# The mixer of an encoder layer: squares summed through transposes, values scaled behind theirs, a new order of work

## The chip, the cores and the metric

The kernel runs on one core of one Trainium2 chip. The core has five engines that work side by side, each through its own queue of instructions in program order: TensorE (matmuls and transposes, written to PSUM), VectorE, ScalarE, GpSimd, and SyncE, which here only issues DMAs. They wait for one another through semaphores. PSUM has eight banks of 128 partitions by 512 float32 numbers. The metric is the time of one execution in microseconds (us), the median of several runs; lower is better.

## What is computed

One layer of an encoder, for 512 positions of 1024 channels in float32: a half-step gated feed-forward network, a mixer, another feed-forward network, a last norm. Only the mixer is touched. It reads, cut to what matters:

```python
def rms_norm(x, g):
    return x * rsqrt(mean(x * x, axis=-1) + EPS) * g

h = rms_norm(x, mix_norm)
u = h @ w_in                  # fourier group (512) | q (8 x 64) | k (2 x 64) | v (2 x 64)
f_out = fourier_mixer(u[..., :512])
q = rms_norm(q.reshape(b, s, 8, 64), q_norm)     # each head by itself
k = rms_norm(k.reshape(b, s, 2, 64), k_norm)
q, k = apply_axial_rope(q), apply_axial_rope(k)
p = softmax(q @ k.T / 8)      # four query heads share one key and value head
a_out = p @ v
x = x + concat([f_out, a_out]) @ w_out
```

There are two norms in a row for q and k: that of x over 1024 channels (its factor, one number a position, is called 1/rms below, `n1.r` in the kernel) and that of each head over its 64 channels.

## The kernel before

Activations lie transposed: channels on the partitions, the 512 positions along a row. Every matmul operand is split into a high and a low part, and a product is three matmuls (high with high, high with low, low with high). The feed-forward networks run before and after the mixer, with TensorE at work without a break.

The mixer is written as some 630 small named operations, and a string `ORDER` (line 47) names them in the order in which they are issued; each engine's queue is this order cut to its own operations, on all five engines. Names that matter below:

- `wk.r`, `wk.h`, `wk.l` (and `wq0` to `wq3`, `wv`, `f0` to `f3`, `fw`, `o0` to `o7`): a weight's load by SyncE into one of three raw buffers, its high part (a cast, mostly on ScalarE) and its low part (a subtraction on VectorE). High and low go into one of three pairs of ring slots, which come free when TensorE is done with the weight that was there.
- `k.0` to `k.7`, `q0.0` to `q3.7`, `v.0` to `v.7`: the eight steps of a projection, three matmuls each.
- `k.sq`, `q0.sq` ...: ScalarE squares the projected bank. `pq`: the squares summed over each head's 64 channels. `s0`, `s1`, `s2`: the sum made into a factor (`s1` is a power of -1/2 on GpSimd).
- `sw`, `sd`, `rc`, `rs`: the rotary step. `ah`, `al`, `bh`, `bl`: the queries' high and low parts. `kw`, `kp`, `km`: the key's factor spread over its channels, transposed, multiplied in. `k0.0` to `k1.3`: the key's parts.
- `vt`, `vp`: the values scaled, transposed to positions on the partitions; `v0.h`, `v0.l`, `v1.h`, `v1.l`: their parts.
- `n1.c`, `n1.m`, `n1.p`: the squares of x summed over the channels, made a mean, and a power -1/2 on GpSimd. `n1.t`, `n1.b`: 1/rms transposed to a row that lies on all partitions, copied to SBUF.
- `s`, `m`, `e`, `t`, `h`, `l`, `v` with three digits (queries, head, block): scores, their maximum (VectorE), exponential (ScalarE), four transposes, the high and low part, product with the values. `o`, `z`, `r`: the attended values gathered, the softmax sums (their reciprocal `z0.r`, spread by GpSimd in `z0.w`, transposed in `z0.p`), the result.
- `f00.0` ... , `map`, `d`, `c`: the Fourier branch; `y0.0` to `y7.7`: the output projection, with the start of the next norm.

Before, the projected q, k and v are not yet multiplied by 1/rms. A head's factor is worked out from the summed squares: times 1/rms twice, divided by 64, EPS added, power -1/2, times 1/rms and (for q) 1/8. So `s0` and `s2` need `n1.p`, and `vt` needs the row of `n1.b`. The sums of squares are matmuls with two columns: the squares are the weights, `halves` (ones in one half of the partitions, zeros in the other) or `ones` the moving operand.

Banks are handed out in the order of the string (`bank_for` takes the first spare one, `read` gives it back), so the order also decides which operation waits for whose bank. Temporary tiles rotate in the same way.

Of the kernel before, what the change touches and what calls it, by code (L numbers as in the profile page):

```python
# [6 lines left out]
F32 = mybir.dt.float32  # L7
# [14 lines left out]
HD = 64  # L22
EPS = 1e-6
# [27 lines left out]
wq3.h q0.bl pos vt wq3.l k1.2 q0.pq q1.1 q1.2 q0.s0 k1.0 k1.1 k1.3 vp q1.3 q1.4 q1.5 q1.6 q1.7 k0.0 k0.2 v0.h  # L51
k0.1 f1.r k0.3 s001 s000 q0.s1 q1.sw q0.s2 v0.l f0.h q1.sd s002 s010 m001 q1.sq q1.pq s003 q2.0 q2.1 q2.2 q2.3
m002 m010 q1.s0 e010 q2.4 q2.5 e001 q2.6 f0.l v1.h q2.7 m003 m000 e002 e003 s011 e000 t000 t001 h001 q1.rc
q1.rs v1.l q3.0 q2.sw f1.h f1.l m011 l001 h000 l000 q2.sd q2.sq t002 s012 m012 h002 fw.r l002 q1.ah q1.al
q2.rc q3.1 q3.2 q3.3 q3.4 q3.5 q3.6 q3.7 q1.bh q1.bl e012 s100 e011 s102 q2.rs q3.sw q3.rc s013 m013 t003 f2.h
q2.bh q1.s1 q1.s2 v000 v001 f00.0 f2.l v002 q3.sq m100 q2.pq e013 q3.sd m102 h003 l003 t010 q2.ah q2.al e100
t013 e102 s101 m101 e101 f00.1 q2.bl f00.u t011 h011 v003 q2.s0 s103 t012 q3.rs q3.bh l011 f02.0 m103 s110
q3.pq h010 l010 v010 v011 o00.c o00.a s201 h012 l012 s111 e103 q3.s0 t100 q3.bl h013 l013 q3.ah t102 h100 m110
v012 v013 o01.c f3.r f02.1 h102 l100 s112 q3.s1 m111 e111 o01.a t101 s113 z0.r z0.w l102 f01.0 h101 e110 m112
z0.p l101 q2.s1 v100 e112 v101 m113 e113 s203 s200 t103 r0.m r0.h f02.e h103 f02.h z1.r q3.s2 q2.s2 m200 z1.w  # L60
e200 l103 r0.l t110 h110 t112 q3.al f01.1 v102 m203 v103 o10.c m201 f01.u l110 o0.r s202 m202 h112 f03.0 o10.a
f03.1 f3.h v110 f03.e t113 e201 t111 f03.h s210 f3.l f03.l f10.0 f10.1 o1.r l112 s211 h111 l111 v111 h113 v112
e203 f10.u l113 s212 m210 m211 e202 t200 m212 t202 s300 f02.l e210 t201 h202 l202 e211 v113 m300 h200 f12.0
h201 l200 l201 f12.1 fw.h fw.l s213 m213 e212 s301 t203 o11.c z1.p v200 v201 v202 o11.a r1.m f12.e e213 t210
s303 h203 l203 e300 t211 h210 f11.0 h211 r1.h m301 l210 l211 s302 f12.h t212 v203 e301 m303 o20.c f13.0 m302
r1.l e302 f12.l s311 f11.1 h212 o20.a m311 z2.r t213 v210 f13.1 l212 s310 o0.h o0.l o3.r map0 o2.r h213 f11.u
l213 e303 t300 t302 f13.e o1.h m310 o1.l v211 v212 v213 t301 f13.h e310 f13.l d00 o21.c o21.a d10 map1 h302
z2.w l302 z2.p map0.h map0.l t303 h300 e311 s312 map1.h l300 v300 r2.m d20 h303 o2.h m312 d01 map1.l s313 d11
h301 l303 l301 v301 m313 d0.h d0.l v302 v303 c0.s e312 e313 t312 t311 o2.l d1.h d1.l o30.c c0.q c0.c d21 h312
# [16 lines left out]
def encoder(ctx, tc, A, out):  # L86
# [660 lines left out]
    with tc.tile_pool(name="mix", bufs=1) as mp, tc.tile_pool(name="mixt", bufs=1) as mt:  # L747
# [132 lines left out]
        def heads_ops(name, t, factor):  # L880

            v = sc[:, :, 2 * t : 2 * t + 2]
            rx = n1.r.unsqueeze(2).to_broadcast([P, 4, 2])

            @op(f"{name}.pq")
            def _():
                banks[f"pq{name}"] = pq = bank_for(f"pq{name}")
                for c in range(4):
                    nc.tensor.matmul(
                        pq[:, 2 * c : 2 * c + 2], sqs[name][:, c * P : (c + 1) * P], halves, start=True, stop=True  # L890
                    )

            @op(f"{name}.s0")
            def _():
                pq = banks[f"pq{name}"][:, 0:8].rearrange("p (c t) -> p c t", t=2)
                nc.vector.tensor_tensor(out=v, in0=pq, in1=rx, op=ALU.mult)
                read(f"pq{name}")
                nc.vector.tensor_tensor(out=v, in0=v, in1=rx, op=ALU.mult)
                nc.vector.tensor_scalar(out=v, in0=v, scalar1=1.0 / HD, scalar2=EPS, op0=ALU.mult, op1=ALU.add)

            @op(f"{name}.s1")
            def _():
                nc.gpsimd.tensor_tensor(out=v, in0=v, in1=mhalf.rearrange("p (c t) -> p c t", t=2), op=ALU.pow)

            @op(f"{name}.s2")
            def _():
                nc.vector.scalar_tensor_tensor(out=v, in0=v, scalar=factor, in1=rx, op0=ALU.mult, op1=ALU.mult)

        qa, qb = {}, {}

# [52 lines left out]
        @op("vt")  # L963
        def _():
            rots["v"] = tp.tile([P, S], F32, tag="g", name="vt")
            nc.vector.tensor_tensor(out=rots["v"], in0=banks["v"], in1=n1.rb, op=ALU.mult)
            read("v")

        @op("vp")
        def _():  # L970
            banks["vp"] = vp = bank_for("vp", 2)
# [3 lines left out]
        def value_ops(v):  # L975


            def own():
                return banks["vp"].rearrange("p (c v e) -> p c v e", c=4, v=2)[:, :, v, :]

            op(f"v{v}.h")(lambda: nc.scalar.copy(vst[:, v, :, 0, :], own()))

            @op(f"v{v}.l")
            def _():
                lows(vst[:, v, :, 1, :], own(), vst[:, v, :, 0, :])
                read("vp")

        for v in range(2):
            value_ops(v)

        for i in range(4):
# [279 lines left out]
        scale = HD**-0.5  # L1275
# [3 lines left out]
        heads_ops("k", 0, 1.0)  # L1279
        key_ops()  # L1280
        for t in range(4):
            query_ops(t)
            heads_ops(f"q{t}", t + 1, scale)
# [18 lines left out]

        @op("n1.c")
        def _():
            banks["ss"] = bank_for("ss")
# [17 lines left out]
        def _():  # L1323
            nc.scalar.copy(n1.rb, banks["rp"])
            read("rp")


        @op("pos")
        def _():
# [237 lines left out]
```

## Time and profile before

| | |
|---|---|
| median of 3 runs | 826.89 us (826.85 to 827.06) |
| the profiled execution | 827.06 us |
| its span in the profile | 824.8 us |
| granted TensorE clock, mean | 0.999 |
| TensorE busy | 816.9 us |
| VectorE busy | 639.2 us |
| ScalarE busy | 464.6 us |
| GpSimd busy | 30.7 us |

The span is the time from the first to the last instruction; the execution has 2.3 us around it. Engines are named PE (TensorE's matmuls), PEld (its weight loads, which overlap them), DVE (VectorE), ACT (ScalarE), POOL (GpSimd) and SP (SyncE) in the profile, and L889 is line 889 of the kernel. A row of a group reads: line, engine, operation, output<-inputs, shapes, xcount | busy time in all, mean ns of one | idle time of the engine before them, and who ended it. A row of the timeline reads: start, duration, engine, line, operation. A row of waits reads: who <- waited for whom: time in all, times, longest. Consecutive operations of an engine overlap in part, so what one costs in a full queue is the distance from its start to the next start.

### The profile page before, as it was taken

To read this page: it belongs to the slowest core of one execution; us is meant where nothing else is said; L and a number is where in the kernel's file an instruction comes from. 1 tells how busy PE (TensorE), PEld (TensorE's weight loads), DVE (VectorE), ACT (ScalarE), POOL (GpSimd) and SP (SyncE) were. 2 spreads that over 40 slices of the span, in tenths; PEclk is the share of its full clock that TensorE was granted. 3 is DMA by queue.
4 is the path that set the end of the run, shared out by engine and by line. 5 is a ranking of instruction groups with operands and counts; after the bars stand their busy time and mean duration, and the time that the engine had idled before them with its cause. 6 is when DMAs were issued, how large, how long until landed. Compare 5 with 4: busy or idle time off the path is not lost.

```text
span 824.8 us, 13679 instructions
## 1 busy us (share of the span) xinstructions
PE 816.9 (99%) x5406; PEld 750.4 (91%) x5406; DVE 639.2 (78%) x1005; ACT 464.6 (56%) x778; POOL 30.7 (4%) x34
## 2 busy tenths in 40 slices
PE   9999999999999999999999999999999999999997
PEld 7889999899989998888999888899988999899986
DVE  7998896489756947699998488998955896479574
ACT  7764664167524645677786357556632674256462
POOL 0110000000000000221100000100000000000001
PEclk9999999999999999999999999999999999999999
DMA  7664322323242213522020224453232332422222
GB/s 256 180 145 173 122 91 77 122 103 141 78 140 102 64 55 115 184 93 77 26 77 27 82 97 116 119 163 123 90 122 94 128 116 63 138 103 97 69 77 103
DMA packets 31168, 89.58 MB, mean 109 GB/s; under 512 B 3712, under 2 KB 8832, under 8 KB 31104
## 3 DMA queue, kind: packets, MB, share of 16 engines
q1 hardware_dynamic: 27776, 82.61, 29.2%
q0 software_dynamic: 2608, 5.12, 3.4%
q8 instruction: 42, 0.69, 0.3%
q10 hardware_dynamic: 720, 0.98, 0.3%
q14 instruction: 22, 0.18, 0.1%
HBM read 84.24 MB, written 2.10 MB: 105 GB/s over the span
## 4 chain that ended last, share of the span: by engine, by line
PE 92%; DVE 5%; issue 1%; ACT 0%; DMA 0%; POOLq 0%; POOL 0%; DVEq 0%; ACTq 0%
PE dn L183 25%; PE r L419 23%; PE q L419 12%; PE gu L183 8%; PE mix L183 7%; PE p L419 6%; PE gu L708 3%; PE mix L1219 1%; PE mix L1176 1%; DVE mx L1156 1%; PE mix L1073 1%; DVE pl L127 1%; PE mix L1015 1%; PE mix L1016 1%; PE mix L1014 1%
## 5 line engine op out<-in xcount | busy, mean ns | idle before, releaser
L419 PE MATMUL r<-rt,ring 128*128 128x256 f32 x1686 | 209.2, 276 | 0.0
L183 PE MATMUL dn<-at,ring 128*128 128x512 f32 x900 | 203.3, 381 | 0.5 <-DVE ring L127 0.4
L419 PEld LDWEIGHTS r<-rt,ring 128*128 128x128 f32 x1686 | 200.3, 188 | 0.8
L183 PEld LDWEIGHTS dn<-at,ring 128*128 128x128 f32 x900 | 168.0, 188 | 29.8 <-DVE ring L127 1.6
L419 PE MATMUL q<-rt,ring 128*128 128x256 f32 x840 | 106.6, 276 | 0.0
L127 DVE TENSOR_TENSOR ring<-s,ring 128x1024 fp32r<-128x1024 f32 x70 | 85.4, 1220 | 24.1 <-ACT ring L378 20.8
L419 PEld LDWEIGHTS q<-rt,ring 128*128 128x128 f32 x840 | 100.4, 188 | 0.0
L543 DVE SCALAR_TENSOR_TENSOR gx<-dn,gx 128x512 f32<-128x512 f32 x61 | 41.9, 688 | 67.6 <-PE dn L183 67.6
L378 ACT CAST ring<-s 128x1024 fp32r<-128x1024 f32 x70 | 73.5, 1050 | 28.0 <-PE p L419 13.7
L169 ACT CAST ring<-raw_dn 128x768 fp32r<-128x768 f32 (+3 forms) x58 | 45.2, 783 | 71.3 <-PE dn L183 62.1
L127 DVE TENSOR_TENSOR ring<-raw_dn,ring 128x768 fp32r<-128x768 f32 (+3 forms) x58 | 51.5, 891 | 5.6 <-PE r L419 4.4
L419 PE MATMUL p<-rt,ring 128*128 128x256 f32 x420 | 53.3, 276 | 0.0
L127 DVE TENSOR_TENSOR ring<-raw_g,ring 128x1024 fp32r<-128x1024 f32 x35 | 42.7, 1219 | 11.1 <-PE p L419 10.2
L419 PEld LDWEIGHTS p<-rt,ring 128*128 128x128 f32 x420 | 50.2, 188 | 0.0
L183 PE MATMUL gu<-ring 128*128 128x512 f32 x216 | 48.9, 381 | 0.0
L183 PEld LDWEIGHTS gu<-ring 128*128 128x128 f32 x216 | 40.4, 188 | 6.9
L378 ACT CAST ring<-raw_g 128x1024 fp32r<-128x1024 f32 x35 | 36.8, 1051 | 16.0 <-DMA raw_g<-in_wgu 8.8
L427 ACT COPY p<-r 128x256 f32<-128x256 f32 x35 | 12.9, 370 | 46.7 <-PE r L419 46.3
L451 ACT ACTIVATE g<-g 128x512 f32<-128x512 f32 x35 | 22.2, 633 | 23.4 <-DVE g L450 23.1
L387 ACT CAST ring<-raw_u 128x512 fp32r<-128x512 f32 x35 | 21.8, 624 | 16.6 <-PE q L419 16.0
L255 POOL TENSOR_TENSOR r<-ms,mhalf 128x4 f32<-128x4 f32 (+1 forms) x4 | 4.3, 1072 | 659.5 <-DVE ms L248 659.5
L464 DVE TENSOR_TENSOR u<-g,u 128x512 f32<-128x512 f32 x35 | 24.0, 685 | 6.1 <-ACT u L463 6.0
(271 smaller groups left out, 1323.1 us busy)
## 6 DMA issues: line engine op xcount, KB each, us to landing
raw_g<-in_wgu SPq DMA_DIRECT2D x35, 512.0 KB, 3.6
raw_u<-in_wgu SPq DMA_DIRECT2D x35, 512.0 KB, 4.3
raw_dn<-in_wd SPq DMA_DIRECT2D x40, 384.0 KB, 3.1
raw_gu<-in_wgu SPq DMA_DIRECT2D x12, 512.0 KB, 3.5
raw_o<-in_wo SPq DMA_DIRECT2D x8, 512.0 KB, 3.5
raw_dn<-in_wd SPq DMA_DIRECT2D x8, 448.0 KB, 3.4
raw_wq<-in_wins SPq DMA_DIRECT2D x4, 512.0 KB, 5.1
raw_f<-in_winf SPq DMA_DIRECT2D x4, 512.0 KB, 4.1
```

Source lines behind the costliest of these rows:

```text
L127: nc.vector.tensor_tensor(out=lo, in0=src, in1=asf(hi), op=ALU.subtract)
L169: nc.scalar.copy(hi[:, :n, :], raw[:, :n, :])
L183: nc.tensor.matmul(ps, a, b, start=first and b is mhi and a is whi, stop=last and a is wlo)
L378: nc.scalar.copy(hi, src)
L387: nc.scalar.copy(hi, src)
L419: nc.tensor.matmul(ps[:, t], a[:, ks], b[:, i, t], start=first and i == 0 and o == 0, stop=i == KH - 1 and o == 2, skip_group_check=not first,
L427: nc.scalar.copy(t, ps)
L451: nc.scalar.activation(b["g"], b["g"], AF.Silu)
L464: nc.vector.tensor_tensor(out=u, in0=b["g"], in1=u, op=ALU.mult)
L543: nc.vector.scalar_tensor_tensor(out=x[d][:, t], in0=ps[:, t], scalar=0.5, in1=x[d][:, t], op0=ALU.mult, op1=ALU.add)
L708: nc.tensor.matmul(turned(pss[c]), w[:, k % 2, c], turned(m[k]), start=k == 0 and m is hh and w is hi, stop=k == KD - 1 and w is lo,)
L1014: nc.tensor.matmul(ps, hh[k][:, cs], whi[:, a, :], start=k == 0, stop=False)
```

## The change

The sums of squares no longer go through two-column products. TensorE transposes the squares, four blocks of 128 x 128 into one bank, and VectorE sums along the row: in `pq` and `s0` for each head's 64 channels, in `n1.c` and `n1.m` for the norm of x (that is, 128 of the partial sums, over which the eight blocks of channels have been added up before).

The head's factor is worked out without 1/rms: sum of squares + 64 EPS (mean of x squared + EPS), power -1/2. This is the whole factor of q; for k a factor of 8 is applied in `kw`. So the steps `s2` go, and `s0` needs only `n1.m` (which also writes the new tile `eps_ms`), not `n1.p`.

The values are copied by ScalarE (`vt`), transposed, and then multiplied by 1/rms (`vs`, VectorE), which is now a number of each partition; `v.h` and `v.l` split both heads at once, from SBUF instead of from PSUM. The row of 1/rms (`n1.t`, `n1.b`) goes.

The string `ORDER` is replaced by another; it has 625 names for 633. Its first part, where it differs most in kind:

```diff
-wk.r wq0.r wv.r wk.h wk.l wq0.h k.0 cos k.1 wv.h wq1.r wq0.l k.2 k.3 wv.l wq2.r k.4 k.5 k.6 k.7 k.sw k.rc k.rs
-q0.0 f0.r q0.1 q0.2 q0.3 k.sq n1.c n1.m wq1.h n1.p wq1.l q0.4 q0.5 q0.6 q0.7 wq2.h q0.rc v.0 wq3.r q0.sw wq2.l
-q1.0 k.pq k.s0 f2.r q0.rs q0.ah v.1 v.2 v.3 q0.sq q0.bh k.s1 k.s2 kw q0.al v.4 v.5 v.6 kp km n1.t n1.b v.7
...
+wq0.r wk.r wv.r wk.h pos wq0.h wk.l k.0 k.1 k.2 k.3 wq1.r k.4 wq1.h k.5 k.6 k.7 wv.h n1.c k.sq wq0.l q0.0
+q0.1 q0.2 cos k.pq wq1.l n1.m q0.3 q0.4 k.sw f3.r q0.5 wv.l wq2.r k.s0 q0.6 k.s1 k.rc q0.7 q1.0 wq2.h k.rs
+q1.1 q1.2 q1.3 q0.rc q0.sq kw f1.r wq2.l kp v.0 q0.sw km k0.2 q0.pq k0.0 k1.0 q0.s0 v.1 q1.4 q0.rs k1.3 q1.5
+v.2 wq3.r k0.1 v.3 q0.bh q1.6 k0.3 q1.7 q2.0 q0.ah q1.sq q0.al s000 v.4 q0.bl v.5 wq3.h s001 s002 s003 q0.s1
...
```

```diff
-        room(mp, 32)
+        eps_ms = mp.tile([P, 8], F32, name="eps_ms")[:, :4]
...
-            rx = n1.r.unsqueeze(2).to_broadcast([P, 4, 2])
+            er = eps_ms.unsqueeze(2).to_broadcast([P, 4, 2])
...
-                    nc.tensor.matmul(
-                        pq[:, 2 * c : 2 * c + 2], sqs[name][:, c * P : (c + 1) * P], halves, start=True, stop=True
-                    )
+                    nc.tensor.transpose(pq[:, c * P : (c + 1) * P], sqs[name][:, c * P : (c + 1) * P], ident)
...
-                pq = banks[f"pq{name}"][:, 0:8].rearrange("p (c t) -> p c t", t=2)
-                nc.vector.tensor_tensor(out=v, in0=pq, in1=rx, op=ALU.mult)
+                pq = banks[f"pq{name}"].rearrange("p (c t e) -> p c t e", c=4, t=2)
+                nc.vector.tensor_reduce(out=v, in_=pq, axis=AX.X, op=ALU.add)
                 read(f"pq{name}")
-                nc.vector.tensor_tensor(out=v, in0=v, in1=rx, op=ALU.mult)
-                nc.vector.tensor_scalar(out=v, in0=v, scalar1=1.0 / HD, scalar2=EPS, op0=ALU.mult, op1=ALU.add)
+                nc.vector.tensor_tensor(out=v, in0=v, in1=er, op=ALU.add)
...
-            @op(f"{name}.s2")
-            def _():
-                nc.vector.scalar_tensor_tensor(out=v, in0=v, scalar=factor, in1=rx, op0=ALU.mult, op1=ALU.mult)
...
-                nc.vector.tensor_copy(kw, sc[:, :, 0:2].unsqueeze(3).to_broadcast([P, 4, 2, HD]))
+                nc.vector.tensor_scalar(
+                    out=kw, in0=sc[:, :, 0:2].unsqueeze(3).to_broadcast([P, 4, 2, HD]),
+                    scalar1=HD**0.5, scalar2=None, op0=ALU.mult,
+                )
...
-            nc.vector.tensor_tensor(out=rots["v"], in0=banks["v"], in1=n1.rb, op=ALU.mult)
+            nc.scalar.copy(rots["v"], banks["v"])
...
+        @op("vs")
+        def _():
+            nc.vector.tensor_tensor(
+                out=rots["v"].rearrange("p (c e) -> p c e", c=4),
+                in0=banks["vp"].rearrange("p (c e) -> p c e", c=4),
+                in1=n1.r.unsqueeze(2).to_broadcast([P, 4, P]), op=ALU.mult,
+            )
+            read("vp")
...
+        op("v.h")(lambda: nc.scalar.copy(vst[:, :, :, 0, :], values()))
+        op("v.l")(lambda: lows(vst[:, :, :, 1, :], values(), vst[:, :, :, 0, :]))
...
             for c in range(4):
-                n1.sum(banks["ss"], c, [n1.acc])
+                nc.tensor.transpose(ss[:, c * P : (c + 1) * P], n1.acc[:, c * P : (c + 1) * P], ident)
...
-            n1.mean(banks["ss"], 0, 4)
+            nc.vector.tensor_reduce(out=n1.ms, in_=banks["ss"].rearrange("p (c e) -> p c e", c=4), axis=AX.X, op=ALU.add)
             read("ss")
+            nc.vector.tensor_scalar(out=n1.ms, in0=n1.ms, scalar1=1.0 / D, scalar2=EPS, op0=ALU.mult, op1=ALU.add)
+            nc.vector.tensor_scalar(out=eps_ms, in0=n1.ms, scalar1=HD * EPS, scalar2=None, op0=ALU.mult)
...
-        @op("n1.t")
-        def _():
-            banks["rp"] = bank_for("rp")
-            for c in range(4):
-                n1.turn(banks["rp"], c)
-
-        @op("n1.b")
-        def _():
-            nc.scalar.copy(n1.rb, banks["rp"])
-            read("rp")
```

More of the change, by code (lines that the diff above doesn't have):

```diff
@@ L53 @@
[L53 to L57, printed above, removed]
@@ new lines @@
+q2.sw s012 q3.3 f0.l f1.h t000 e010 q2.sd e011 q2.rc m012 t003 vs q2.sq h000 fw.r t001 s013 e012 s102 t002
+f1.l m102 q3.4 v.h q3.5 h002 q3.6 f00.0 l000 s100 m013 h001 l002 v.l l001 e013 e102 q3.7 q2.pq f2.h m100 v000
+q3.sw z0.r q3.sd t010 q2.s0 q1.bh q2.s1 v001 q2.rs f01.0 e100 f2.l s101 f00.1 q2.ah h010 m101 q3.sq f02.0
+q1.bl l010 o2.r s103 v002 e101 f02.1 h003 t011 q3.rc q2.bh f00.u l003 h011 m103 q2.bl v003 t013 f02.e e103
+t012 o0.r q3.rs q3.pq s112 v010 q3.ah l011 f01.1 q2.al s110 q3.s0 h012 h013 s113 l012 v011 o00.c o00.a l013
@@ new lines @@
+m113 m112 s212 e113 m110 f03.0 f01.u e112 m212 q3.al o1.r t103 f03.1 f3.h t101 h101 v012 q3.s1 h103 f03.e
+l101 v013 e212 t100 h100 o01.c f10.0 f3.l l103 fw.h s213 l100 q3.bh f12.0 o01.a s111 f03.h f10.1 f02.h q3.bl
+t102 f10.u f03.l e110 s210 s211 h102 v100 m213 z0.w e213 f02.l m111 v101 e111 s201 m210 m211 f12.1 o5.r l102
+f12.e e211 z0.p r0.m t111 t112 v102 h111 h112 fw.l l112 v103 o10.c s203 f12.h e210 t110 f11.0 h110 m201 l111
+o4.r m203 f13.0 o10.a t113 o0.h s202 t210 f12.l e203 l110 f11.1 v110 r0.h o0.l h113 s200 f11.u m202 f13.1
@@ new lines @@
+d3.h c0.l m313 c2.c h300 v202 e313 c1.l v203 y0.0 o20.c m310 h301 l300 c2.o y0.1 e310 d3.l l301 o20.a z2.w
+z3.r y1.0 y1.1 c2.h t303 v300 o2.h c3.s c3.c t310 v301 c3.q o7.r t302 c2.l y1.2 h310 h303 c3.o h302 y0.2 l302
+t312 z2.p c3.h v302 c3.l t311 h311 l310 l303 y1.3 y1.4 o6.r z3.w r1.h l311 t313 v310 y0.3 h313 o2.l v303
+o30.c r1.l y2.0 y1.5 v311 y2.1 h312 l313 l312 r2.m v312 v313 z3.p o30.a y2.2 y0.4 r2.h o31.c r2.l o31.a y1.6
+y0.5 r3.m y0.6 r3.h y2.3 r3.l y0.7 y2.4 o3.h y2.5 y2.6 o3.l y1.7 y2.7 y1.x y3.0 o5.h o5.l y3.1 y3.2 y2.x y0.x
@@ L78 @@
+y3.3 y2.q o4.h y5.0 y3.4 o4.l y3.5 y5.1 y0.q y1.q y3.6 y5.2 y5.3 y3.7 y5.4 y5.5 y4.0 y5.6 y4.1 y3.x y4.2 o6.h
+y1.h y4.3 y2.h y5.7 y4.4 o6.l y4.5 o7.h y5.x y0.h y6.0 y5.h y4.6 y3.h y1.l y1.a o7.l y3.q y6.1 y2.l y5.q y4.7
+y7.0 y4.x y4.q y3.l y7.1 y6.2 y2.a y7.2 y4.h y6.3 y5.l y6.4 y6.5 y3.a y0.l y7.3 y6.6 y6.7 y4.a y5.a y7.4 y6.x
+y4.l y7.5 y6.h y6.l y6.q y7.6 y7.7 y7.x y6.a y7.q y7.h y7.a y7.l
 """
@@ L878, in _, with heads_ops @@
                 nc.vector.tensor_tensor(out=r, in0=r, in1=sw, op=ALU.add)
-        def heads_ops(name, t, factor):
+        def heads_ops(name, t):
             v = sc[:, :, 2 * t : 2 * t + 2]
-            rx = n1.r.unsqueeze(2).to_broadcast([P, 4, 2])
+            er = eps_ms.unsqueeze(2).to_broadcast([P, 4, 2])
             @op(f"{name}.pq")
@@ L970, in _, with values @@
         def _():
-            banks["vp"] = vp = bank_for("vp", 2)
+            banks["vp"] = vp = bank_for("vp")
             for c in range(4):
                 nc.tensor.transpose(vp[:, c * P : (c + 1) * P], rots["v"][:, c * P : (c + 1) * P], ident)
[L975 to L983, printed above, removed]
-            def _():
[L985 to L989, printed above, removed]
+        @op("vs")
[6 more added lines that the diff above has]
+            read("vp")
+        def values():
+            return rots["v"].rearrange("p (c v e) -> p v c e", c=4, v=2)
+        op("v.h")(lambda: nc.scalar.copy(vst[:, :, :, 0, :], values()))
+        op("v.l")(lambda: lows(vst[:, :, :, 1, :], values(), vst[:, :, :, 0, :]))
         for i in range(4):
@@ L1278, in encoder @@
         rope_ops("k", qkg[:, 1:2])
-        heads_ops("k", 0, 1.0)
+        heads_ops("k", 0)
         key_ops()
```

35 lines of the change are left out of this document (9 added, 26 removed).

## The prediction

> **What bounds the kernel now.** I read the page first: the engines' shares, the granted clock, the chain of work that ended last.
>
> ```profile
> span 824.8 us, 13679 instructions
> PE 816.9 (99%) x5406; PEld 750.4 (91%) x5406; DVE 639.2 (78%) x1005; ACT 464.6 (56%) x778; POOL 30.7 (4%) x34
> ...
> PEclk9999999999999999999999999999999999999999
> ...
> PE 92%; DVE 5%; issue 1%; ACT 0%; DMA 0%; POOLq 0%; POOL 0%; DVEq 0%; ACTq 0%
> ```
>
> TensorE is at work all the way at the full clock, and 92% of the chain is TensorE; but a share over the whole span says nothing of the mixer, which alone is edited. The timeline puts its first product (`k.0`) at 330.9 us, and in the chain its last block of projections, 40.30 us from 449.72, ends at 490.03. So I read busy time by windows of it (TensorE, weight loads, VectorE, ScalarE, GpSimd, clock, DMA):
>
> ```profile
> 331.00:350.00 19.00, 19.00 (x100) 16.51 (x99) 13.32 (x22) 13.26 (x19) 4.45 (x5) 1.00 0.59 189
> 350.00:375.00 25.00, 25.00 (x133) 21.49 (x132) 24.08 (x48) 18.80 (x36) 4.71 (x2) 1.00 0.31 98
> 375.00:400.00 25.00, 24.72 (x177) 22.64 (x176) 23.89 (x55) 18.96 (x41) 4.96 (x4) 1.00 0.15 50
> 400.00:425.00 25.00, 25.00 (x188) 23.37 (x188) 23.59 (x49) 19.46 (x41) 0.61 (x1) 1.00 0.13 43
> 425.00:450.00 25.00, 25.00 (x169) 22.89 (x168) 23.30 (x44) 19.16 (x39) 0.61 (x1) 1.00 0.17 64
> ```
>
> TensorE has no hole but 0.28 us. VectorE is a close second from 350 to 450 us: 24.08 + 23.89 + 23.59 + 23.30 = 94.9 of 100 us. In the first 19 us it has 5.7 us to spare, and after 450 us it idles. What TensorE waited for in 331 to 490 us, as the idle time of its weight loads, is all of this:
>
> ```profile
> PEld mix L1150 <- ACT e L1164: 0.4, 1, 0.4
> PEld mix L1150 <- DVE pl L127: 0.4, 1, 0.4
> PEld mix L1176 <- ACT e L1164: 0.2, 1, 0.2
> ```
>
> So the mixer is bound by TensorE's list of work. An edit there is worth what it takes off that list, plus at most 1.0 us of waits, minus what a new order makes TensorE wait.
>
> **TensorE's own work.** Three kinds of groups have to be priced: four two-column products, four transposes between other work, and the four transposes of the 1/rms row.
>
> ```profile
> 357.67 0.39 PE L1151 MATMUL mix<-ks,near 128*128 128x512 f32 x1
> 357.91 0.95 PE L889 MATMUL mix<-halves,sq_q 128*128 128x2 f32 x8
> 358.71 0.47 PE L1150 MATMUL mix<-ks,near 128*128 128x512 f32 x1
> ...
> 393.22 0.60 PE L1208 MATMUL mix<-ident,zw 128*128 128x128 f32 x4
> 393.57 0.47 PE L1219 MATMUL mix<-ph,near 128*128 128x512 f32 x1
> ...
> 348.57 0.60 PE L946 MATMUL mix<-ident,kw 128*128 128x128 f32 x4
> 349.00 0.60 PE L260 MATMUL mix<-ident,r 128*128 128x128 f32 x4
> 349.36 0.92 PE L183 MATMUL mix<-ring,more 128*128 128x512 f32 x3
> ```
>
> Busy times overlap, so a group costs the distance from its start to the next start: 358.71 - 357.91 = 0.80 us for the products (the count of 8 shows that each runs twice, and each run loads 128 columns of weights), 393.57 - 393.22 = 0.35 us for transposes of the same 128 x 512 data. Six groups change over (`n1.c`, `k.pq`, `q0.pq` to `q3.pq`): 6 x 0.45 = 2.7 us. The row's transposes (`n1.t`) go: 0.36 to 0.43 us by the two rows, I take 0.4. The values' transposes (`vp`) stay. Together 3.1 us. That the squares' transposes cost what `z0.p`'s do is no guess: same shape, same identity. The bounds are 0 (they pay what the products paid) and 0.45 each.
>
> The idle-free busy time of the weight loads gives a second price:
>
> ```profile
> L889 PEld LDWEIGHTS mix<-halves,sq_q 128*128 128x128 f32 x32 | 4.2, 191 | 0.3
> L889 PEld LDWEIGHTS mix<-halves,sq_k 128*128 128x128 f32 x8 | 1.0, 190 | 0.1
> L241 PEld LDWEIGHTS mix<-ones,acc 128*128 128x128 f32 x8 | 1.0, 191 | 0.1
> L260 PEld LDWEIGHTS mix<-ident,r 128*128 128x128 f32 x4 | 0.5, 137 | 0.0
> ```
>
> 4.2 + 1.0 + 1.0 + 0.5 = 6.7 us of loads go and six groups at 0.5 come: 3.7 us instead of 3.1. I take 3.1, since distances between starts are what TensorE's list adds up to, and keep 3.7 as the other bound. The Trainium skill (Perfetto Trace Analysis, Identifying the Most-Contended Engine) holds that the matmuls' busy time tells little of how full TensorE is, and that the weight loads' busy time is to be read; by it 3.7 would be the sum's term, and the result 822.2.
>
> **VectorE, ScalarE, GpSimd.**
>
> ```profile
> L1156 DVE TENSOR_REDUCE mx<-mix 128x1 f32<-128x512 f32 x32 | 21.9, 683 | 1.0 <-PE mix L1151 0.9
> L899 DVE TENSOR_SCALAR sc<-sc 128x8 f32<-128x8 f32 x5 | 0.9, 173 | 0.2
> L898 DVE TENSOR_TENSOR sc<-sc,r 128x8 f32<-128x8 f32 x5 | 0.8, 169 | 0.2
> L896 DVE TENSOR_TENSOR sc<-mix,r 128x8 f32<-128x8 f32 x5 | 0.8, 161 | 0.1
> L966 DVE TENSOR_TENSOR vt<-mix,rb 128x512 f32<-128x512 f32 x1 | 0.7, 691 | 0.0
> L127 DVE TENSOR_TENSOR near<-mix,near 128x256 fp32r<-128x256 f32 x2 | 0.8, 414 | 0.0
> L907 DVE SCALAR_TENSOR_TENSOR sc<-sc,r 128x8 f32<-128x8 f32 x5 | 0.7, 149 | 0.0
> L1324 ACT COPY rb<-mix 128x512 f32<-128x512 f32 x1 | 0.6, 585 | 0.0
> L981 ACT CAST near<-mix 128x256 fp32r<-128x256 f32 x2 | 0.7, 370 | 0.0
> ```
>
> Each head's `s0` and `s2` lose 161 + 169 + 173 + 149 = 652 ns and gain a sum over a bank and one small add. A sum into eight columns is in no row; the nearest is the maximum over a bank, 683 ns; bounds are the sum of a few columns (161) and two such passes (1366). I take 683 + 169 = 852, so +0.2 us a head, 5 heads. `n1.m` grows by about 0.9 us (one sum and two small steps for one), at about 337 us, where VectorE has time. For the values, 691 + 2 x 414 = 1519 ns become `vs` and `v.l`, two full passes, 2 x 691 = 1382: -0.1 us. `kw` is a copy with a factor in place of a copy: 0, bounds 0 and 0.3 us. ScalarE trades the row's copy (585) for the values' (the same pass) and two half casts (740) for one whole: nothing. GpSimd's five powers stay; none is waited for by a VectorE step of its own now, since the four scaling steps `s2` are gone.
>
> In 350 to 450 us this is 4 x 0.2 - 0.1 = +0.7: 95.6 us of VectorE. TensorE's share shrinks to 100 - 4 x 0.45 - 1.0 = 97.2. VectorE still fits, with 1.6 us over: the cover is thin, and the order decides.
>
> **The new order.** I followed it where another engine's queue comes nearest to TensorE's list, adding rows in queue order.
>
> ```profile
> 327.99 1.23 DVE L127 TENSOR_TENSOR ring<-raw_wk,ring 128x1024 fp32r<-128x1024 f32 x1 [0.17 <-ACT ring L812]
> ...
> 331.95 1.23 DVE L127 TENSOR_TENSOR ring<-raw_wq,ring 128x1024 fp32r<-128x1024 f32 x1 [0.17 <-ACT ring L812]
> ...
> DMA to landing us min/median/max: 3.5/5.1/5.4
> ```
>
> 1. The start. A projection step (3 matmuls) takes 0.66 us, so `k.7` ends at 336.2, and behind `n1.c` and three steps `k.pq` is due at 338.6. It needs `k.sq`, now behind `wq1.h` and `wv.h` on ScalarE (0.95 us each). `wq1`'s load needs a raw buffer: free after `wk.l` at 329.2, landed 5.1 us later at 334.4, cast by 335.4. `wv.h` waits for `k.7` (its ring slots), ends at 337.4; `k.sq` (0.6) at 338.0. 0.6 us to spare. The order of the first two loads costs nothing: now the second is issued at 316.9, 10 us ahead of its cast. `pos`, first on GpSimd, has nothing behind it that is due before 339; its transfers run beside `wq1`'s, for which the same 0.6 and the wait for `k.7` are the cover.
> 2. The first score. 18 steps and 3 groups after `k.pq`, `s000` is due at 351.7. Its operand: `wq2.h` behind `q0.7` ends at 343.4, `q0.sq` 344.0, `q0.sw` (2.7) 346.7, three key casts and two query casts 349.9, and `q0.al` behind `k0.3` on VectorE about 351.5. 0.2 to spare; it saves because the key's factor comes 4 us earlier.
> 3. The values now wait for `n1.p`, on GpSimd behind `q1.s1`: about 362. `vs` stands some 4 us later in VectorE's queue, and `v000` past 373. Nothing waits.
>
> I find no place where TensorE must wait, so the 1.0 us of waits is counted as gained (bounds: 0 gained, or 1.5 lost at three places as thin as 2). Past the mixer the list is the old one.
>
> **Sum:** 3.1 + 1.0 = 4.1 us. The profiled execution took 827.06 us (824.8 of span, 2.3 around it): 823.0. The median of the three runs is 0.17 lower, so 826.89 - 4.1 = **822.8 us**. Its own range is 822.0 to 823.7: 4.7 by the load rows on one side, no wait gained on the other.
>
> **Rivals.**
> - Thin places wait, 0.5 us each at three: 822.8 + 1.5 = 824.3. For it: the 0.2 us at `s000`. Against: 0.6 elsewhere. 15%.
> - `wq1`'s load gets the buffer of `wq0` instead of `wk`'s. `wq0.l` ends at 333.2, so it lands at 338.3 and `k.sq` ends at 340.8 (two casts and the square): `k.pq` waits 2.2. `wq2` then follows `wv.l`, and by the sums of 2 `s000` waits 0.9 more: 822.8 + 3.1 = 825.9. Against: `wk.l` ends 4 us ahead of `wq0.l`. 5%.
> - The change doesn't do what it says: the six groups of transposes pay 0.80. Then 0.4 + 1.0 = 1.4: 825.5. Only the row of `z0.p` speaks, and against it. 4%.
> - Slower: VectorE becomes the bound in 350 to 450 us. It has 95.6 us to do; now it idles 5.1 of 100. If the new order holds it idle for 7.5% of that stretch, this takes 95.6 / 0.925 = 103.4 us, 3.4 over the old 100, less the 1.3 saved ahead of it (`n1.c`, `k.pq`, `n1.t`): 826.89 + 2.1 = 829.0. It decides over the forecast from 97.2 us, over the old time from 101.3 (5.6% idle). For it: the share. Against: two waits of 0.4 us are all that VectorE's and ScalarE's queues cost TensorE now. 6%.
>
> **How the numbers follow.** 70% for 822.8. The measurement tells 0.2% (1.65 us) from no change, so faster is below 825.2: 70 + 15 = 85%. Within: the second and third, 9%. Slower: 6%. The range goes from the load rows' 822.2, rounded down to 822.0, to 825.2, past the thin places.
>
> **What would show it.** Each of the six groups of transposes is followed by its next start within 0.35 to 0.45 us; TensorE's mixer ends 4 us earlier after its start, near 486; no weight load waits over 0.3 us; the sums over a bank last about 0.68 us; VectorE's share in the stretch rises from 95% to 97 or 98%. I would be wrong if a load of `wq1` lands after 336, if weight loads wait for VectorE again and again between 350 and 400, or if the sums cost twice the maximum's.

## The result, and the profile after

The changed kernel took 824.41 us in the median of 6 runs (823.36 to 824.96); the kernel before, beside it, 826.97 (6 runs, 826.71 to 827.52). The ratio is 0.9967 [0.9954, 0.998]: 2.6 us faster. The profiled execution took 823.36 us, 3.7 less than the one of before.

The page of the changed kernel: span, busy time of each engine, and the share of each in the chain of work that ended last.

```profile
span 821.1 us, 13621 instructions
...
PE 814.0 (99%) x5378; PEld 747.0 (91%) x5378; DVE 640.8 (78%) x996; ACT 464.5 (57%) x777; POOL 30.6 (4%) x34
...
PE 97%; DVE 1%; issue 1%; DMA 0%; ACT 0%; POOLq 0%; POOL 0%; DVEq 0%
```

The shares of busy time hardly moved. The chain did: VectorE had 5% of it and has 1%. The 5% were some 41 us (of 824.8), and the pieces of the chain of before between 350 and 392 us add up to 34.5 us of VectorE and 1.5 of TensorE. Seven microseconds of the chain, by line, before and after:

```profile
by line: DVE mx L1156 26.2%; DVE more L127 16.2%; DVE rot_q L869 12.7%; DVE sw_q L877 10.0%; DVE pl L127 10.0%; DVE rot_q L878 9.9%; DVE near L127 9.8%; issue 8.7%; DVE mx L1157 5.0%; DVE sc L907 1.1%
```

```profile
by line: PE mix L1008 18.1%; PE mix L1007 18.1%; PE mix L1006 18.0%; PE mix L1211 13.1%; PE mix L183 9.7%; PE mix L1143 6.3%; PE mix L889 6.2%; PE mix L1168 6.2%; PE mix L1142 6.2%
```

From 371 to 378 us the chain of before holds no TensorE at all; after, nothing else. Busy time in windows does not show this (TensorE, weight loads, VectorE, ScalarE, GpSimd, clock, DMA; the changed kernel):

```profile
331.00:350.00 19.00, 19.00 (x96) 16.23 (x95) 15.37 (x24) 14.30 (x21) 5.38 (x5) 1.00 0.65 227
350.00:375.00 25.00, 24.99 (x134) 21.17 (x133) 23.91 (x46) 17.51 (x35) 3.72 (x3) 1.00 0.24 74
375.00:400.00 25.00, 25.00 (x188) 23.64 (x187) 24.27 (x45) 18.23 (x38) 4.21 (x3) 1.00 0.16 54
400.00:425.00 25.00, 25.00 (x175) 22.90 (x174) 23.59 (x46) 20.98 (x43) 0.62 (x1) 1.00 0.18 64
425.00:450.00 25.00, 25.00 (x157) 22.33 (x156) 22.44 (x49) 18.39 (x37) 1.23 (x2) 1.00 0.06 16
```

From 350 to 450 us VectorE is busy for 94.2 of 100 us, 94.9 before. Ahead of 350 us it does 2 us more than before (15.37 for 13.32): the new order starts its work earlier.

In this text "the mixer's time" is the distance from the start of `k.0` to the start of the first product of the next feed-forward network. On the timeline of before, and then of after:

```profile
330.89 1.48 PE L183 MATMUL mix<-ring 128*128 128x512 f32 x6
...
489.87 1.48 PE L183 MATMUL gu<-ring 128*128 128x512 f32 x6
```

```profile
330.76 2.58 PE L183 MATMUL mix<-ring 128*128 128x512 f32 x11
...
486.42 1.92 PE L183 MATMUL gu<-ring 128*128 128x512 f32 x8
```

158.98 us before and 155.66 after: 3.3 of the 3.7 us lie in the mixer. Of the rest, 0.13 lie ahead of it, and 0.26 behind it: the column sums of the next norm waited for 0.4 us (this row of the waits of before has no counterpart after). There `y7.l` was issued ahead of the norm's start `y7.a`, and is not now; the kernels below that keep the old order have the wait, and those of the new order do not.

```profile
PEld ss L241 <- issue: 0.4, 1, 0.4
```

Summed over TensorE's starts, the 3.3 us are: `n1.c` from 0.81 to 0.35 and the five `pq` from 4.10 to 1.77, 2.8 us; `n1.t` gone, 0.36; two waits of 0.38 each gone and one of 0.2 new, 0.6. That makes 3.7. Against it 0.4 us came in small parts at projections, output projection and value products. One group of transposes and its next start:

```profile
338.48 0.60 PE L889 MATMUL mix<-ident,sq_k 128*128 128x128 f32 x4
338.84 1.37 PE L183 MATMUL mix<-ring 128*128 128x512 f32 x5
```

338.84 - 338.48 = 0.36 us. The costs of VectorE's new steps, from the groups:

```profile
L894 DVE TENSOR_REDUCE sc<-mix 128x8 f32<-128x512 f32 x5 | 3.5, 690 | 0.8 <-PE mix L889 0.6
L933 DVE TENSOR_SCALAR kw<-sc 128x512 f32<-128x512 f32 x1 | 0.4, 417 | 0.0
L896 DVE TENSOR_TENSOR sc<-sc,eps_ms 128x8 f32<-128x8 f32 x5 | 0.8, 169 | 0.2
```

And all that TensorE's weight loads wait in the mixer:

```profile
PEld mix L1142 <- DVE near L127: 0.4, 1, 0.4
```

That is `s000`. Its product starts 0.2 us late.

### The profile page after: what moved, and what is told of

It reads as the page before. It is cut to its first block, busy times and chain, and to the rows that moved or that the text cites. A ratio compares the mean times of both kernels' runs of the same rounds, so it can differ in the third digit from the quotient of the medians.

```text
span 821.1 us, 13621 instructions
## 1 busy us (share of the span) xinstructions
PE 814.0 (99%) x5378; PEld 747.0 (91%) x5378; DVE 640.8 (78%) x996; ACT 464.5 (57%) x777; POOL 30.6 (4%) x34
## 4 chain that ended last, share of the span: by engine, by line
PE 97%; DVE 1%; issue 1%; DMA 0%; ACT 0%; POOLq 0%; POOL 0%; DVEq 0%
PE dn L183 25%; PE r L419 23%; PE q L419 12%; PE mix L183 9%; PE gu L183 8%; PE p L419 6%; PE gu L708 3%; PE mix L1211 2%; PE mix L1168 2%; PE mix L1142 1%; PE mix L1006 1%; PE mix L1008 1%; PE mix L1007 1%; PE mix L1143 1%; PE mix L1065 1%
## 5 line engine op out<-in xcount | busy, mean ns | idle before, releaser
L183 PE MATMUL mix<-near,ring 128*128 128x512 f32 x120 | 29.7, 383 | 0.0
```

Of the source, the lines that this page charges most:

```text
L183: nc.tensor.matmul(ps, a, b, start=first and b is mhi and a is whi, stop=last and a is wlo)
```

## The experiments

The mixer's time of each profiled execution, start and end from the timeline as above:

| kernel | order | sums by | start, end | mixer | median (runs) | ratio to before |
|---|---|---|---|---|---|---|
| before | old | products | 330.89, 489.87 | 158.98 | | |
| after | new | transposes | 330.76, 486.42 | 155.66 | 824.41 (6) | 0.9967 [0.9954, 0.998] |
| after_again | new | transposes | 333.20, 489.05 | 155.85 | 824.92 (5) | 0.9962 [0.9949, 0.9974] |
| products | new | products | 333.54, 491.62 | 158.08 | 826.65 (11) | 0.9989 [0.9979, 0.9998] |
| old_order | old | transposes | 331.11, 491.80 | 160.69 | 830.08 (6) | 1.0029 [1.0018, 1.004] |
| old_order_products | old | products | 331.06, 489.39 | 158.33 | 826.76 (11) | 0.9993 [0.9984, 1.0001] |
| old_order_both | old | products and VectorE | 333.50, 494.51 | 161.01 | 829.56 (10) | 1.002 [1.0011, 1.003] |
| double_sums | new | transposes, summed twice | 333.35, 491.48 | 158.13 | 827.55 (12) | 1.0 [0.9988, 1.0011] |

Each ratio is to the kernel before, run beside it. Except in before itself, the values take the new path and the head's factor is the shorter one in all of them. The start differs by some 2.4 us between executions of one kernel (after and after_again), ahead of the mixer; the mixer's time differs by 0.2. So the mixers are compared, and the medians beside them.

**after_again**, the changed kernel once more, as a yardstick.

> The changed kernel, unaltered. What is open is the gap between its profiled execution (823.36 us, the lowest of six) and its median (824.41): 1.05 us, while the profile alone accounts for 3.7 us of gain. If the gap lies in the granted clock, the executions spread again by over 1 us, each slower one with a mean clock of 0.998 or 0.999 against 1.000, and the kernel before spreads in the same way. If it lies in the kernel (a load that lands late in some executions), the spread is there at one and the same clock. Either way the median lies between 823.4 and 825.0.

824.92 against 827.77 (24 runs) of the kernel before. Its profiled execution was its slowest, 826.32 us, and what was late there was the start of the mixer, 333.20 for 330.76, not the mixer. The clock does not explain the spread: its mean was 0.999 in this execution, 1.000 in one of 825.07 us and 0.998 in one of 824.63.

**products**: the new order, but the sums by two-column products again.

```diff
-                    nc.tensor.transpose(pq[:, c * P : (c + 1) * P], sqs[name][:, c * P : (c + 1) * P], ident)
+                    nc.tensor.matmul(
+                        pq[:, 2 * c : 2 * c + 2], sqs[name][:, c * P : (c + 1) * P], halves, start=True, stop=True
+                    )
...
-                nc.vector.tensor_reduce(out=v, in_=pq, axis=AX.X, op=ALU.add)
+                nc.vector.tensor_tensor(out=v, in0=pq, in1=er, op=ALU.add)
...
-                nc.tensor.transpose(ss[:, c * P : (c + 1) * P], n1.acc[:, c * P : (c + 1) * P], ident)
+                n1.sum(ss, c, [n1.acc])
```

> The new order and the values' new path, but the squares summed by two-column products again (six groups), with one small addition behind them on VectorE. If TensorE's list of work sets the time, six groups cost 0.45 us more each: 2.7 us over the changed kernel, the distance from a group's start to the next start 0.80. If the order alone brings the gain, it stays within 0.5 us of the changed kernel.

The mixer is 2.4 us longer than after's (158.08). So in the new order the six groups of transposes are worth 2.4 of the 3.3 us, near the 2.8 of their own starts.

**old_order**: the new operations in the old order; `vs` and `v.h` stand where `v0.h` stood, `v.l` where `v0.l` did, and the names that no longer exist are left out. Its beginning:

```diff
-wq0.r wk.r wv.r wk.h pos wq0.h wk.l k.0 k.1 k.2 k.3 wq1.r k.4 wq1.h k.5 k.6 k.7 wv.h n1.c k.sq wq0.l q0.0
...
+wk.r wq0.r wv.r wk.h wk.l wq0.h k.0 cos k.1 wv.h wq1.r wq0.l k.2 k.3 wv.l wq2.r k.4 k.5 k.6 k.7 k.sw k.rc k.rs
...
```

> The new operations in the old order (names that no longer exist left out; the values' scaling and its high part where the first head's high part stood). If TensorE's list sets the time, the 3.1 us of work come off here too, and what is left of the waits (1.0 us before, and about as much again where VectorE's queue was already at its limit and now has 0.2 us more a head) is all that the order is worth: 0.5 to 1.5 us slower than the changed kernel, 1.5 to 3 us faster than the kernel before. If the order brings the gain, it stays within 0.8 us of the kernel before.

A miss: 830.08 us, 2.3 slower than before, although TensorE's list is 3.1 us shorter. The longest waits of its weight loads in the mixer, and the chain from 373 to 380 us by line:

```profile
PEld mix L1141 <- DVE pl L126: 1.0, 1, 1.0
PEld mix L1210 <- DVE pl L126: 1.0, 2, 0.7
PEld mix L1141 <- DVE ks L126: 0.9, 1, 0.9
PEld mix L1167 <- ACT e L1155: 0.8, 1, 0.8
PEld mix L941 <- DVE kw L932: 0.8, 1, 0.8
PEld mix L182 <- DVE ring L126: 0.7, 1, 0.7
```

```profile
by line: DVE mx L1147 26.2%; DVE rot_q L868 18.0%; DVE more L126 16.2%; DVE sw_q L876 10.1%; DVE pl L126 10.0%; DVE rot_q L877 9.9%; DVE near L126 9.9%; DVE mx L1148 5.1%; issue 3.6%; DVEq L1148 0.3%
```

The weight loads wait at nine places, 0.4 to 1.0 us each, mostly for VectorE. Three causes were possible: the place of `n1.m`, the values' new path, or the sums on VectorE.

**double_sums**: the changed kernel, each head's sum over a bank done twice.

```diff
-                nc.vector.tensor_reduce(out=v, in_=pq, axis=AX.X, op=ALU.add)
+                for _ in range(2):
+                    nc.vector.tensor_reduce(out=v, in_=pq, axis=AX.X, op=ALU.add)
```

> The changed kernel with each head's sum over a bank made twice (the second writes the same numbers): five more passes of 0.6 us on VectorE, four of them, 2.4 us, in the stretch from 350 to 450 us where it has about 1.6 us to spare. With TensorE's list as the bound and that much cover, about 0.8 us is lost, as new waits of TensorE's weight loads behind VectorE; if VectorE already is the bound there, all of 2.4 to 3 us; if the cover is larger than counted, under 0.3 us.

```profile
PEld mix L1143 <- DVE sc L895: 1.5, 1, 1.5
PEld mix L1143 <- DVE near L127: 1.0, 1, 1.0
PEld mix L1143 <- DVE vt L974: 0.4, 1, 0.4
PEld mix L1007 <- DVE oo L1227: 0.2, 1, 0.2
```

These are all the waits of its weight loads in the mixer. Five passes of 690 ns are added, 3.45 us, the first of them in the mixer's start, where VectorE has time; the mixer grew by 158.13 - 155.66 = 2.5. So the new order covers 1.0 us of all five, or 0.3 of the other four, not the 1.6 of the prediction's account. A loss of this size was expected if VectorE already set the changed kernel's time. The changed kernel's own chain says that it does not, TensorE alone from 350 to 392 us; but VectorE's is only some 0.3 us short of it.

**old_order_early_mean**: old_order with the mean of the norm early.

```diff
-wk.r wq0.r wv.r wk.h wk.l wq0.h k.0 cos k.1 wv.h wq1.r wq0.l k.2 k.3 wv.l wq2.r k.4 k.5 k.6 k.7 k.sw k.rc k.rs
-q0.0 f0.r q0.1 q0.2 q0.3 k.sq n1.c n1.m wq1.h n1.p wq1.l q0.4 q0.5 q0.6 q0.7 wq2.h q0.rc v.0 wq3.r q0.sw wq2.l
+wk.r wq0.r wv.r wk.h wk.l wq0.h k.0 cos k.1 wv.h wq1.r wq0.l k.2 k.3 wv.l wq2.r k.4 k.5 k.6 k.7 n1.c n1.m k.sw
+k.rc k.rs q0.0 f0.r q0.1 q0.2 q0.3 k.sq wq1.h n1.p wq1.l q0.4 q0.5 q0.6 q0.7 wq2.h q0.rc v.0 wq3.r q0.sw wq2.l
```

> The new operations in the old order, but the squares of x are turned and summed (`n1.c`, `n1.m`) directly behind `k.7`, as in the new order. In the old order with the new operations `n1.m` (0.9 us longer on VectorE) lies between `k.rs` and `wq1.l`, and everything behind it came 0.7 us later. If this place is what made that kernel slow, the waits at `q1.0` (0.6 us) and `kp` (0.6 us) go and most of those at the first scores: the mixer's 160.7 us on TensorE become about 159, and the time falls by 1.5 us or more. If it is the sum of VectorE's longer steps in a queue without slack, wherever they stand, less than 0.8 us comes back.

829.05 us (12 runs), ratio 1.002 [1.0011, 1.0028]; the mixer 160.20. The wait at `q1.0` fell from 0.7 to 0.2 us (weight loads), the others stayed: the place of the mean is worth 0.5 us and is not the cause.

**old_order_products**: old_order with the sums by two-column products, that is, the edit of products above in the old order. Of the change, only the values' path and the shorter factor are left.

> The old order, the values' new path and no row of 1/rms, but the squares summed by two-column products. TensorE's list is 0.4 us shorter than before. If the sums on VectorE made the old order slow with the new operations, this one is at the old kernel's time or up to 0.8 us faster (mixer 158.2 to 159.0 us on TensorE). If the values' path did it (its copy waits on ScalarE's queue, its scaling on GpSimd's power), it keeps 1 us or more of the loss: mixer 160 us or more.

826.76 us; the mixer 158.33, 2.4 us less than old_order's. The page's chain by engine:

```profile
PE 97%; DVE 1%; issue 1%; DMA 0%; ACT 0%; POOLq 0%; POOL 0%; DVEq 0%
```

The values' path is cleared. With the sums on TensorE and without the steps `s2`, even the old order is bound by TensorE's list; it is the sums on VectorE that the old order can't carry.

**old_order_casts_moved**: old_order with the high parts of `f0` and `f1` cast by ScalarE, to take work from VectorE.

```diff
-HI_DVE = ("f0", "f1")
+HI_DVE = ()
```

> The new operations in the old order, with the high parts of `f0` and `f1` cast on ScalarE in place of VectorE (0.6 us each off VectorE's queue at about 357 and 363 us, 1.0 us each onto ScalarE's). If the old order lost because VectorE's queue was full from 341 to 392 us, about 1.2 us of the mixer's 160.7 comes back, at the waits behind 357 us (`s011`, `t013`, `q3.pq`, `t101`); those ahead of it (`v.6`, `q1.7`, `s001`) stay. If it lost through the latency of single chains, or ScalarE is as full, under 0.4 us comes back.

832.01 us (4 runs), ratio 1.0051 [1.0031, 1.0071]; the mixer 162.76, 2.1 longer than old_order's. A miss. The longest wait of VectorE for ScalarE between 345 and 392 us, and the window in which it lies:

```profile
DVE ring L126 <- ACT ring L811: 3.2, 1, 3.2
```

```profile
350.00:375.00 25.00, 22.85 (x112) 18.21 (x111) 20.89 (x38) 18.39 (x34) 4.72 (x2) 1.00 0.35 105
```

The cast came later from ScalarE's queue, and VectorE, which makes the low part from it, stood still for 3.2 us with all that is queued behind. Its busy time fell from old_order's 23.94 to 20.89 of 25 us and the mixer became longer: it is the chain through VectorE's queue that counts, not its load.

**old_order_both**: old_order_products, with a sum over 512 columns on VectorE added in each `s0` and in `n1.m`, whose result is overwritten. TensorE's list stays the long one; VectorE gets the new steps.

```diff
+                nc.vector.tensor_reduce(
+                    out=v, in_=sqs[name].rearrange("p (c t e) -> p c t e", c=4, t=2), axis=AX.X, op=ALU.add
+                )
...
+            nc.vector.tensor_reduce(out=n1.ms, in_=n1.acc.rearrange("p (c e) -> p c e", c=4), axis=AX.X, op=ALU.add)
```

> The old order with two-column products, and beside them on VectorE one sum over 512 columns in each `s0` and in `n1.m` (its numbers are overwritten by the products' sums). So TensorE has the longer list of `old_order_products` (mixer 158.3 us) and VectorE about the work of `old_order` (mixer 160.7 us). If in the old order VectorE's chain sets the time by itself, the mixer takes 160.2 to 161 us here too, with waits of 2 to 3 us in all instead of 5: the longer list only fills what TensorE waited. If the waits of `old_order` come from anything else that the transposes bring (their banks held longer, their place on TensorE), the mixer stays under 159.3 us.

829.56 us; the mixer 161.01 against old_order's 160.69. The page's chain by engine, and that from 373 to 380 us by line:

```profile
PE 92%; DVE 5%; issue 1%; DMA 1%; ACT 1%; DVEq 0%; POOLq 0%; POOL 0%; ACTq 0%
```

```profile
by line: issue 17.7%; DVE mx L1151 17.5%; DVE more L126 16.2%; DVE near L126 13.0%; DVE rot_q L868 10.3%; DVE sw_q L876 10.0%; DVE rot_q L877 9.9%; DVE pl L126 8.6%; DVE mx L1152 4.6%
```

TensorE's products against transposes make no difference (0.3 us); the passes on VectorE, added alone, cost 161.01 - 158.33 = 2.7. That shows the cause: in the old order VectorE's chain sets the mixer's time as soon as it has the sums.

**cos_first**: the changed kernel with `cos` (two loads by SyncE) ahead of `wq1.r`, to test the margin of 0.6 us at the mixer's start.

```diff
-wq0.r wk.r wv.r wk.h pos wq0.h wk.l k.0 k.1 k.2 k.3 wq1.r k.4 wq1.h k.5 k.6 k.7 wv.h n1.c k.sq wq0.l q0.0
-q0.1 q0.2 cos k.pq wq1.l n1.m q0.3 q0.4 k.sw f3.r q0.5 wv.l wq2.r k.s0 q0.6 k.s1 k.rc q0.7 q1.0 wq2.h k.rs
+wq0.r wk.r wv.r wk.h pos wq0.h wk.l k.0 k.1 k.2 k.3 cos wq1.r k.4 wq1.h k.5 k.6 k.7 wv.h n1.c k.sq wq0.l q0.0
+q0.1 q0.2 k.pq wq1.l n1.m q0.3 q0.4 k.sw f3.r q0.5 wv.l wq2.r k.s0 q0.6 k.s1 k.rc q0.7 q1.0 wq2.h k.rs q1.1 q1.2
```

> The changed kernel with the loads of the cosines ahead of `wq1`'s load on SyncE's queue. They wait until the last feed-forward product is done, so `wq1`'s load is issued 2.8 us later (about 331.9 from the old start of the mixer at 330.8). It then lands near 335.5 to 337. By the sum of the start (cast 1.0 us, `wv.h` 1.0, `k.sq` 0.6 behind the landing) `k.sq` ends at 338.0 to 339.6 and `k.pq` is due at 338.5: a wait of 0 to 1.1 us there, none elsewhere, if the new order's start has the 0.6 us to spare that was counted. If the start has none to spare, all of 2.8 us is lost; if a later load is what bounds it, the loss shows behind `k.pq`.

The wait was over three times as long as expected: 829.82 us (one run), the mixer 160.91. Timeline of SyncE, ScalarE and TensorE (in brackets the idle time before, and who ended it), and after it the windows:

```profile
332.25 0.38 SPq L150 DMA_DIRECT2D raw_wq<-in_wins  x1
...
340.06 1.04 ACT L811 CAST more<-raw_wq 128x1024 fp32r<-128x1024 f32 x1 [6.74 <-DMA raw_wq<-in_wins]
...
342.60 0.66 PE L888 MATMUL mix<-ident,sq_k 128*128 128x128 f32 x4 [3.54 <-ACT sq_k L840]
```

```profile
344.00:346.00 2.00, 2.00 (x6) 1.51 (x6) 1.91 (x4) 1.32 (x2) 0.60 (x1) 0.50 0.83 270
```

The load is issued 1.09 us behind the mixer's first product (331.16 here); in the changed kernel it was issued at 329.11, 1.65 ahead of it. So it is 2.7 us later, and it lands 7.7 us after its issue instead of 3.5; ScalarE idles until then. `k.pq` waits 3.54 us, and behind that the granted clock is 0.50 for a while, which adds another 1.7 us. What the same load had to spare in the changed kernel, from ScalarE's timeline (the casts of `wq1.h` and `wv.h`, the square):

```profile
332.83 1.03 ACT L812 CAST more<-raw_wq 128x1024 fp32r<-128x1024 f32 x1
...
336.06 1.05 ACT L812 CAST ring<-raw_wv 128x1024 fp32r<-128x1024 f32 x1 [2.19 <-issue]
337.01 0.59 ACT L841 ACTIVATE sq_k<-mix 128x512 f32<-128x512 f32 x1
```

2.19 us stand between the casts, and the square ends at 337.60, 0.88 ahead of `k.pq` at 338.48: 3.1 us. The load lands 2.7 + 4.2 = 6.9 us later, less 3.1 makes 3.8. Measured from the mixer's first product, `k.pq` starts 11.44 us behind it instead of 7.72, 3.7 us later.

**cos_first_late_tables**: the same, with GpSimd's loads of the tables (`pos`) put behind `k.s1`.

> As the kernel with the cosines' loads first, but the Fourier tables' loads (`pos`, 1.4 MB in all) stand on GpSimd behind `k.s1`, as they did before the change. In the kernel with the cosines first, `wq1`'s load took 7.7 us beside them and `k.pq` waited 3.5 us. If the tables' transfers took the bandwidth, `wq1`'s load now takes 3.5 to 5 us, `k.pq` waits at most 1.1 us, and no step of a projection runs at half the clock behind it: the mixer takes 155.7 to 157 us on TensorE. If the load is slow for another reason, the wait stays over 2.5 us.

As expected: the load, as late as in cos_first, landed in 4.9 us, `k.pq` started 0.92 us late (2.7 + 1.4 - 3.1 = 1.0), the mixer took 156.85, and the one run 827.34. So 2.8 of the 7.7 us came from the tables' 1.4 MB on GpSimd's queue beside the load.

**n2_turned**: the changed kernel, with `s000` one step later (behind `v.4`), and the next norm's column sums by four transposes and a sum on VectorE as well.

```diff
+            if self.n == 2:
+                for c in range(4):
+                    nc.tensor.transpose(ps[:, c * P : (c + 1) * P], parts[0][:, c * P : (c + 1) * P], ident)
+                nc.vector.tensor_reduce(out=self.ms, in_=ps.rearrange("p (c e) -> p c e", c=4), axis=AX.X, op=ALU.add)
```

> The changed kernel with two more edits: the first score `s000` one projection step later (behind `v.4`), and the next norm's column sums, at the end of the mixer, by transposes and a sum on VectorE too. If TensorE's list sets the time and both have cover (VectorE idles for over 2 us behind those sums, the power is due 2.7 us after them), the wait at `s000` (0.2 us) goes and the group of sums costs 0.35 instead of 0.80 us: 0.6 us off the changed kernel's profile, no new wait at the row of 1/rms. If the longer chain (sum, mean, power) is not covered, TensorE waits at that row and the gain is 0.2 us or less.

824.9 us (5 runs), ratio 0.9967 [0.9955, 0.9979]: no faster than the changed kernel. The mixer took 155.71: the wait at `s000` is gone, but its 0.2 us are no more than the mixer differs by between two executions. The group itself went from 0.80 to 0.36 us, as its starts show, but later in that network a product waited for VectorE:

```profile
491.46 0.60 PE L235 MATMUL ss<-ident,acc 128*128 128x128 f32 x4
491.82 0.93 PE L182 MATMUL gu<-ring 128*128 128x512 f32 x3
...
532.63 0.79 PE L182 MATMUL dn<-at,ring 128*128 128x512 f32 x1 [1.98 <-DVE ring L126]
```

```profile
533.00:536.00 3.00, 3.00 (x8) 2.32 (x8) 3.00 (x7) 1.76 (x3) 0.00 (x0) 0.50 0.50 133
```

The wait is 1.98 us here and 0.43 in the changed kernel's profile, and the clock is halved for 3 us behind it. It goes back to a weight's load, for which ScalarE's cast waits:

```profile
526.93 1.05 ACT L385 CAST ring<-raw_g 128x1024 fp32r<-128x1024 f32 x1 [3.08 <-DMA raw_g<-in_wgu]
```

The load was issued at 521.8 us in both kernels and landed after 5.1 us here, after 3.5 in the changed kernel: 1.6 us later, and the wait is 1.55 longer. So the wait is not the work of the edit on VectorE. The profiled execution was the slowest of the five (826.09 us); whether the others had this wait is open.

## Why the prediction was right, and where it was not

**The time and the sign.** 822.8 was predicted and 824.41 measured, inside the range. (The range's own bound with no wait gained is 826.89 - 3.1 = 823.8, not 823.7.) 4.1 us were to go; 3.7 went between the two profiles, 2.6 between the medians. Why the medians differ less than the mixers (by 0.7; 2.9 in the second comparison, by 0.4) is open.

**TensorE's own work: right.** 3.1 us by the distances between starts, and 2.8 + 0.36 were found. The weight loads' row would have given 3.7; the starts were the better measure.

**The waits: mis-sized.** 1.0 us was counted as gained, 0.6 was. The third wait of before, 0.2 us for ScalarE, cost TensorE's list nothing, and `s000`, with its margin of 0.2, waits 0.2 (0.4 for the weight load, where no wait over 0.3 was foretold). The prediction's account had the place right and the sign of so small a margin wrong.

**Nothing else in the mixer: mis-sized, by 0.4.** The sum has no term for the other products, and many became slower by a few hundredths each. Most of this is in the kernel products too, which has the new order without the transposes: by the distances between starts, the output projection takes 0.29 us more than before in both, the value products 0.34 after and 0.32 in products. So it came with the order; why is open.

**VectorE's costs: right in size.** A sum over a bank was put at 683 ns and took 690; `kw` took 417; the values waited for nothing. The load of `wq1` got the buffer of `wk`. VectorE's share from 350 to 450 us was to rise to 97 or 98% and is 94%: the sums made its work longer (639.2 us before, 640.8 after, over the span), but the new order does 2 us more of it ahead of 350 us.

**The step that failed** is "So the mixer is bound by TensorE's list of work. An edit there is worth what it takes off that list, plus at most 1.0 us of waits, minus what a new order makes TensorE wait." For the changed kernel it holds, whose chain is TensorE alone from 350 to 392 us. For the kernel before it does not, and neither does the worth of the edit that is drawn from it. The four mixers of the table:

| | products | transposes | gain of the transposes |
|---|---|---|---|
| old order | 158.33 | 160.69 | -2.4 |
| new order | 158.08 | 155.66 | +2.4 |
| gain of the order | 0.25 | 5.0 | |

In the old order the same groups, shorter by 2.8 us on TensorE, made the mixer longer. The kernel before had two chains of nearly the same length from 350 to 392 us, and the one that ended last ran through VectorE. TensorE waited for only 1.0 us in all, because its own list was nearly as long, not because VectorE had time. The row for this was in the prediction's first fence, DVE 5% of the chain, 41 us; it was passed over, since "a share over the whole span says nothing of the mixer", and the chain was not read for the stretch that is edited. The time came out because the order was changed together with the sums, and the prediction followed that order at its thin places. That the cover was enough is in part luck: it counted 1.6 us, and double_sums finds 0.3.

The rival "VectorE becomes the bound" (829.0, 2.1 us slower than before) is what happened when the order was not changed with the sums: 2.3 us slower, by VectorE's chain. That the two numbers are so near is chance, as the rival's was worked out for the new order. There it did not come, with little to spare. A sum of busy time over a stretch of 100 us counts free time that lies where it can't be used.

By the Trainium skill (Perfetto Trace Analysis, Identifying the Most-Contended Engine) the engine with the highest occupancy is to be improved first, TensorE judged by its weight loads. In 350 to 375 us of before these are 21.49 / 25 = 86%, VectorE 24.08 / 25 = 96%. So the rule names VectorE, and old_order agrees. For the changed kernel it also names VectorE (85% and 96%), and there its chain holds TensorE alone: two engines this close are told apart by the chain and by the order of their queues, not by their occupancy.

**The start: right, with more to spare.** The prediction left the square 0.6 us and the load 1.65 (1.05 between the casts and 0.6). 0.88 and 3.1 were found, as the load landed in 3.5 us instead of 5.1. Its cover for the tables beside the load held because the load is issued early: cos_first shows what the same transfers cost when it is not.

## What to carry to other kernels

Read the chain of waits for the stretch that is edited before saying what bounds it: an engine with 5% of the chain may hold most of it for 40 us. Where two engines are near full, as here, moving work from the one to the other can be worth less than nothing by itself; it pays together with an order that starts the second engine's chain earlier, and the way to see this is the four kernels of a table with and without each edit. A change that gains a few us is measured by the time of its own stage, since the start of that stage wandered here by 2.4 us, nearly as much as the gain.

## What the runs showed of the hardware

The granted clock fell to 0.50 for some 3 us after TensorE had waited 3.54 us (cos_first), and also after a wait of 1.98 us (n2_turned). After a wait of 1.10 us (double_sums) it stayed at 1.00. The Trainium skill (TensorE: Matmul & The Clock Gate, What's actually happening) puts the halving at an idle window of about 3.4 us that runs by itself. The first wait is as long as that window, which agrees; the second is shorter, and there the measurement decides. So a wait of 2 us can cost more than itself.

A load of 512 KB took 4.9 us without GpSimd's table loads beside it (cos_first_late_tables) and 7.7 with them (cos_first), one execution each.
